# Four edits to a hybrid decoder block on one core: where NSA's masks are added, the layout of compression's tokens, the first transfers, and mLSTM's values

## The chip, the cores and the metric

The kernel runs on one core of a Trainium2 chip. The engines are PE (TensorE, matmuls), ACT (ScalarE), DVE (VectorE), POOL (GpSimd) and SP (SyncE, which here only issues transfers). The metric is the time of one execution in device microseconds; the time given is the median of three runs.

## The reference

One layer of a decoder block in fp32: 256 tokens of width 1024, 256 memory tokens. Three mixers run on the normalised input, their outputs are gated, summed and projected, and a SwiGLU channel mixer follows.

```
z = rmsnorm(x) @ w_in                      # q, 6 x kv, gates, mLSTM's q k v, merge gates
# NSA: 16 heads of 64 in 4 groups; three softmaxes for each head and token
kc, vc = compress(k0), compress(v0)        # 15 overlapping blocks of 32 tokens: silu(blocks @ w1 + pe) @ w2
o_cmp = softmax(q kc^T masked: block's end <= token) vc
o_slc = softmax(q k1^T masked: causal) v1  # 4 selection blocks, top 16: all of them
o_win = softmax(q k2^T masked: causal) v2  # the window of 512 covers all 256 tokens
y_nsa = g0 o_cmp + g1 o_slc + g2 o_win
# mLSTM, 4 heads of 128: a gated linear attention, num / max(|den|, exp(-m)), rms-normed per head
# memory cross-attention: 4 heads of 128 over rmsnorm(mem) @ w_mem_kv
y = sum_b sigmoid(merge_b) * (y_b @ w_proj_b);  x = x + rmsnorm(y @ w_out)
x = x + rmsnorm((silu(h @ w_gate) * (h @ w_up)) @ w_down),  h = rmsnorm(x)
```

## The kernel before, in words

fp32 products are made of three matmuls in fp32r: each operand is split into a high part (`whi`, `hh`, written by ACT) and the rest (`wlo`, `hl`, by DVE), and hi x hi, hi x lo and lo x hi are added in PSUM. The weights come in 162 units of 512 KB (`raw`, four buffers), each split once (`split`), so ACT and DVE each have a pass of 1024 columns for every unit.

All instructions are first recorded by `Plan` and then put in order by its own list scheduler, one fixed order for each engine. `Plan.cost` gives each instruction a duration in ns; a DVE pass costs 71 + 1.04 ns a column, whatever its operation. Priorities, `FIRST`, and a search over small shifts set the order; all profile lines therefore carry the line of `issue` (L597), and rows are told apart by tile names.

The start: SP issues the gain and first chunk of the memory (`m0`, 264 columns), the first weight unit, further chunks (`memt`) and units. Ten fp32 matmuls on ones (`warm_up`) run meanwhile, two records each. Then eight chunks of 128 channels of the memory's keys (`mem_k`) are multiplied, each with four matmuls for each of the three products (`kps`, shown as `pd<-mh,whi` and so on). `HEAD` says in how many pieces a unit's split is made.

Compression (`ph`): for keys and values (j = 0, 1) the tile `st` holds the 4 groups' tokens one after the other on 64 partitions and the same shifted by one token on the other 64. For each of 16 pairs of positions one plain fp32 matmul loads 80 columns of it at a step of 16 tokens and moves 128 columns of `w1`; the result lies token-major, is copied by ACT (`hs`), transposed by PE (`pht`), and goes on to the silu.

NSA's softmax (`nsa_half(g, tb)`, 4 groups and two halves of 128 tokens): for each of 4 heads PE makes the scores `sc` of the three branches, 272 columns for the first half, 272 and 256 in two banks for the second (16 compressed, then selected and window keys), each from two matmuls. The masks are added on PE, as matmuls of the bf16 identity (`identb`) with the bf16 mask: one of 272 columns for a head's first half, three (128, 16 and 128) for its second. DVE then takes three maxima for each head (`mx`), ACT the three exponentials with their sums, DVE scales them, PE transposes (`ptn`), ACT and DVE split (`pTh`, `pTl`), and PE multiplies by the values (`pvn`). Two heads share one scaling. Between the halves other tasks are recorded as filling: mLSTM's projections, its heads and the merge gates.

mLSTM's heads (`ml_head`): the weights `sh`, `sl` (hi and lo) of two token blocks times the values; `vml` holds values hi and values lo in separate planes, each of 128 columns and two of ones (which give the denominator). The second token block has two source blocks, so a head takes 3 x 3 matmuls of 130 columns into `pn`.

Of the kernel before, what the change touches and what calls it, by code (L numbers as in the profile page):

```python
# [12 lines left out]
F32 = mybir.dt.float32  # L13
# [14 lines left out]
N_UNITS = 162  # L28
HEAD = (2, 2, 1, 1)
# [9 lines left out]
K_ID, K_TRI, K_RV, K_BM, K_M0, K_C1, K_MT, K_END = 0, 128, 256, 257, 261, 533, 549, 677  # L39
# [5 lines left out]
class View:  # L45
# [21 lines left out]
    def rearrange(self, pattern, **sizes):  # L67
# [12 lines left out]
        assert [n for g in sides[0] for n in g] == [n for g in sides[1] for n in g]  # L80
# [6 lines left out]
        ix = self.ix.reshape([math.prod(sizes[w] for w in g) for g in sides[1]])  # L87
# [80 lines left out]
class Plan:  # L168
# [68 lines left out]
    def cost(op):  # L237
# [40 lines left out]
    FIRST, DRAIN, PLACE = 5000.0, 4000.0, 200.0  # L278
# [322 lines left out]
def block_kernel(ctx, tc, order, xN, xT, memN, memT, cst, vec, row, wg, w1, w2, W, out):  # L601
# [151 lines left out]
    memt = bigt("G", 3, [P, KD, S], F32, "memt")  # L753
# [11 lines left out]
    m0 = work.tile([P, KD + S], F32, tag="sq", bufs=3, name="m0")  # L765

    def mem_in(k):
        gain = m0[:, k:k + 1]
        src = memt[:, k, :] if k else m0[:, KD:]
        ACT.activation(mh[:, k, :], src, AF.Copy, scale=gain)  # L770
# [3 lines left out]
    def keep_k(i, ps):  # L774
# [7 lines left out]

    fetch(("mem_k", 0))
    dma(out=m0, in_=memT[:, 0:KD + S])
    mem_dma = lambda a, b: dma(out=memt[:, a:b, :], in_=memT[:, KD + a * S:KD + b * S].rearrange(
        "p (k s) -> p k s", k=b - a))
    mem_dma(1, 4)
    fetch(("mem_k", 1))
    mem_dma(4, 8)
    warm_up(10)  # L790
# [3 lines left out]
    for u in range(4):  # L794
        if ("mem_k", u) not in ready:
            fetch(("mem_k", u))
        raw = ready.pop(("mem_k", u))
# [54 lines left out]
    mraw = work.tile([P, K_END - K_M0], F32, tag="sq", bufs=3, name="mraw")  # L852
# [7 lines left out]
    dma(out=mraw, in_=cst[:, K_M0:])  # L860
# [5 lines left out]
    msk = one.tile([P, 416], BF16, name="msk")  # L866
    DVE.tensor_copy(msk, mraw)
    M0, MC1, MT, MD = msk[:, 0:272], msk[:, 272:288], msk[:, 288:416], msk[:, 0:P]
# [4 lines left out]
    for j in range(2):  # L873

        sf = bigt("E", 2, [P, 5 * S + 32], F32, f"st{j}")
        st = sf[:, 0:5 * S].rearrange("p (g t) -> p g t", g=5)
        POOL.memset(sf[:, 4 * S:], 0.0)
        POOL.memset(st[64:128, 0:4, S - 1:S], 0.0)
        POOL.tensor_copy(sf[:, 4 * S:4 * S + 32:2], vc[:, V_PEK + 16 * j:V_PEK + 16 * j + 16])
# [5 lines left out]
        ph = ps_v([80, P], "ph")  # L885
        for l in range(16):
            PE.matmul(ph, sf[:, 2 * l:2 * l + 16 * 79 + 1:16], w1t[j][:, l, :], start=(l == 0), stop=(l == 15))
        hs = work.tile([80, P], F32, tag="junk", bufs=2, name="hs")
        ACT.activation(hs, ph, AF.Copy)
        pht = ps_t([P, 80], "pht")  # L890
        PE.transpose(pht, hs, cs[0:80, K_ID:K_ID + 80])
        bias = work.tile([P, 1], F32, tag="b1", bufs=2, name="cbias")
        DVE.tensor_copy(bias, pht[:, 64:65])
        ACT.activation(hid[:, j, :, 0:NCMP], pht[:, 0:64].rearrange("p (g n) -> p g n", g=NG)[:, :, 0:NCMP], AF.Silu,
# [189 lines left out]
    vml = bigt("G", 3, [P, 2, 2, 4, P + 2], F32R, "vml")  # L1084
# [439 lines left out]
```

## Time and profile before

| | |
|---|---|
| runs | 549.79, 551.13, 549.82 us; median 549.82 |
| profiled execution | 550.37 us, its span from first to last instruction 548.6 us |
| granted clock of TensorE | 0.998 over the span |
| busy: PE, DVE, ACT, POOL | 539.8, 411.6, 343.0, 26.5 us |
| transfers | 97.8 MB, 178 GB/s on the mean |

Rows of the profile have start and duration in us, engine, line, operation, output<-inputs, shapes and count. A matmul's duration reaches from its start until its last result, and the next one starts long before that. PEld is PE's loading of weights. Waits are named by the engine that released them.

### The profile page before, as it was taken

Reading aid. Unit: us, or ns where it says so; the run is one execution under the profiler, and the core shown is the slowest. Engines: PE = TensorE matmul, PEld = TensorE weight load, DVE = VectorE, ACT = ScalarE, POOL = GpSimd, SP = SyncE. Lnnn points to the kernel's source line nnn. Section 1 sums busy time; section 2 is a strip of 40 time slices with the busy share of each in tenths; the row PEclk is TensorE's granted clock in tenths of the full one; section 3 lists DMA queues with packets and bytes.
Section 4 is the critical chain, followed back from the end, with each engine's and each line's share of the span. In section 5 each row is a group of like instructions: output and inputs, shape, how many; then the busy total and the mean of one; then the engine's idle time right before and its main releaser. Section 6 shows DMA issues by size and latency. Waiting matters only on the chain.

```text
span 548.6 us, 8855 instructions
## 1 busy us (share of the span) xinstructions
PE 539.8 (98%) x3194; PEld 474.8 (87%) x3194; DVE 411.6 (75%) x799; ACT 343.0 (63%) x676; POOL 26.5 (5%) x43
## 2 busy tenths in 40 slices
PE   9999999999999999999999999999999999999995
PEld 8899998998989889889888888788888888888884
DVE  5795696699989898987878697975777777754543
ACT  7684696576699775965896444754555555553431
POOL 0000000010020111102110000000000000000000
PEclk9999999999999999999999999999999999999999
DMA  8995326526323445345345565654455555555512
GB/s 312 416 396 198 114 107 202 194 79 229 116 79 116 147 176 178 115 154 193 112 157 177 206 217 191 226 173 148 159 192 193 191 189 184 192 185 182 189 70 76
DMA packets 28699, 97.80 MB, mean 178 GB/s; under 512 B 3312, under 2 KB 5488, under 8 KB 28400
## 3 DMA queue, kind: packets, MB, share of 16 engines
q1 hardware_dynamic: 28656, 97.24, 49.7%
q8 instruction: 25, 0.41, 0.3%
q14 instruction: 18, 0.15, 0.1%
HBM read 95.13 MB, written 1.05 MB: 175 GB/s over the span
## 4 chain that ended last, share of the span: by engine, by line
PE 91%; ACT 3%; DMA 2%; DVE 1%; issue 1%; POOL 1%; DVEq 0%; SPq 0%; ACTq 0%
PE pd L597 48%; PE pss L597 30%; PE sc L597 3%; PE pvn L597 2%; DMA raw<-in_W 2%; PE ph L597 2%; PE ptn L597 2%; ACT whi L597 1%; PE pn L597 1%; PE psm L597 1%; PE pgf L597 1%; PE pvm L597 1%; POOL ce L597 1%; PE ptx L597 0%; ACT L597 0%
## 5 line engine op out<-in xcount | busy, mean ns | idle before, releaser
L597 DVE TENSOR_TENSOR wlo<-raw,whi 128x1024 fp32r<-128x1024 f32 (+1 forms) x160 | 194.6, 1222 | 85.7 <-ACT whi L597 84.0
L597 ACT ACTIVATE whi<-raw 128x1024 fp32r<-128x1024 f32 (+1 forms) x160 | 167.3, 1049 | 131.8 <-PE pd L597 65.7
L597 PE MATMUL pd<-hh,wlo 128*128 128x256 f32 x208 | 59.6, 286 | 0.0
L597 PE MATMUL pd<-hl,whi 128*128 128x256 f32 x208 | 59.5, 286 | 0.0
L597 PE MATMUL pd<-hh,whi 128*128 128x256 f32 x208 | 59.3, 285 | 0.0
L597 PE MATMUL pd<-wlo,hh 128*128 128x512 f32 x144 | 58.4, 406 | 0.0
L597 PE MATMUL pd<-whi,hh 128*128 128x512 f32 x144 | 58.2, 404 | 0.0
L597 PE MATMUL pd<-whi,hl 128*128 128x512 f32 x144 | 57.0, 401 | 0.0
L597 PE MATMUL pss<-xc,whi 128*128 128x512 f32 x168 | 43.2, 392 | 0.0
L597 PE MATMUL pss<-whi,u 128*128 128x512 f32 x132 | 42.4, 392 | 0.0
L597 PEld LDWEIGHTS pd<-hh,whi 128*128 128x128 f32 x208 | 39.7, 191 | 0.4 <-DVE on L597 0.2
L597 PEld LDWEIGHTS pd<-hl,whi 128*128 128x128 f32 x208 | 39.8, 191 | 0.1
L597 PEld LDWEIGHTS pd<-hh,wlo 128*128 128x128 f32 x208 | 39.7, 191 | 0.1
L597 PEld LDWEIGHTS pss<-xc,whi 128*128 128x128 f32 x168 | 30.7, 189 | 5.4
L597 PE MATMUL pd<-xc,whi 128*128 128x512 f32 x120 | 31.9, 394 | 0.0
L597 PEld LDWEIGHTS pd<-wlo,hh 128*128 128x128 f32 x144 | 27.2, 189 | 4.4
L597 PEld LDWEIGHTS pd<-whi,hl 128*128 128x128 f32 x144 | 27.2, 189 | 4.3
L597 PEld LDWEIGHTS pd<-whi,hh 128*128 128x128 f32 x144 | 27.2, 189 | 4.2
L597 PEld LDWEIGHTS pss<-whi,u 128*128 128x128 f32 x132 | 24.8, 188 | 5.5
L597 ACT ACTIVATE pp<-sc,mx 128x128 f32<-128x128 f32 (+1 forms) x64 | 26.8, 431 | 1.0 <-DVE mx L597 0.8
L597 DVE TENSOR_REDUCE mx<-sc 128x1 f32<-128x16 f32 (+2 forms) x96 | 22.8, 288 | 6.1 <-PE sc L597 5.9
L597 PE MATMUL pss<-wlo,u 128*128 128x512 f32 x66 | 25.9, 392 | 0.0
(334 smaller groups left out, 1129.9 us busy)
## 6 DMA issues: line engine op xcount, KB each, us to landing
raw<-in_W SPq DMA_DIRECT2D x162, 512.0 KB, 3.2
w<-in_w SPq DMA_DIRECT2D x2, 1024.0 KB, 7.6
xn<-in_xN SPq DMA_DIRECT2D x2, 512.0 KB, 7.3
xt<-in_xT SPq DMA_DIRECT2D x2, 512.0 KB, 8.7
mn<-in_memN SPq DMA_DIRECT2D x2, 512.0 KB, 8.2
kk<-kk SPq DMA_DIRECT2D x8, 128.0 KB, 3.3
x<-in_xN SPq DMA_DIRECT2D x2, 512.0 KB, 3.7
memt<-in_memT SPq DMA_DIRECT2D x1, 512.0 KB, 7.6
```

The source lines that it names most:

```text
L597: op.ins_ = getattr(op.real, op.method)(*map(arg, op.a), **{k: arg(x) for k, x in op.kw.items()})
```

## The change

Four edits, and two planner constants (`FIRST`, the cost of an fp32 matmul).

- NSA's masks: the mask matmuls go. The masks stay in fp32 in SBUF (`msk`), and each of the three reductions of a head becomes one `tensor_tensor_reduce` on DVE, which writes -(score + mask) over the score in PSUM and the minimum of it to `mx`; the exponential uses scale -1.
- Compression: `st` is laid out with the position within a block outermost, so that 80 tokens stand at step 1. `w1` is loaded, the tokens move, the result has the hidden width on the partitions, and the copy `hs` and the transpose `pht` go. ACT's copies into `st` become four of 256 columns for each of keys and values, and DVE's shifted copies two (960 and 63 columns).
- First transfers: gain, first memory chunk and first weight unit are joined with the rest of the memory in one array (`head`), fetched in four pieces; the first has 776 columns. Two warm-ups fewer, the first chunk's hi part on DVE, the order of the three products changed.
- mLSTM: values hi, ones, values lo stand side by side (258 columns), so that `sh` meets all of them in one matmul; the lo part is added by DVE after a copy by ACT.

```diff
-K_ID, K_TRI, K_RV, K_BM, K_M0, K_C1, K_MT, K_END = 0, 128, 256, 257, 261, 533, 549, 677
+K_ID, K_TRI, K_RV, K_BM, K_M0, K_MC, K_MT, K_END = 0, 128, 256, 257, 261, 645, 677, 805
-HEAD = (2, 2, 1, 1)
+HEAD = (2, 2, 2, 1)
...
-                return max(2.05 * op.a[1].n, n / 0.6 + 10)
+                return max(1.72 * op.a[1].n, n / 0.6 + 10)
-    FIRST, DRAIN, PLACE = 5000.0, 4000.0, 200.0
+    FIRST, DRAIN, PLACE = 4300.0, 4000.0, 200.0
...
+    mt = bigt("KK", 1, [P, 3080], F32, "memt")
+    part = lambda a, b: dma(out=mt[:, a:b], in_=head[:, a:b])
...
-        ACT.activation(mh[:, k, :], src, AF.Copy, scale=gain)
+        if k == 0:
+            DVE.tensor_scalar(mh[:, k, :], src, gain, None, op0=ALU.mult)
+        else:
+            ACT.activation(mh[:, k, :], src, AF.Copy, scale=gain)
...
-    fetch(("mem_k", 0))
-    dma(out=m0, in_=memT[:, 0:KD + S])
-    mem_dma(1, 4)
+    part(0, 776)
+    part(776, 1544)
     fetch(("mem_k", 1))
-    mem_dma(4, 8)
-    warm_up(10)
+    part(1544, 2056)
+    fetch(("mem_k", 2))
+    part(2056, 3080)
+    warm_up(8)
...
-            for i, (x, y) in enumerate(((w[0], mh), (w[1], mh), (w[0], ml))):
+            for i, (x, y) in enumerate(((w[0], mh), (w[0], ml), (w[1], mh))):
...
+        st = bigt("E", 2, [P, 16, 96], F32, f"st{j}")
...
         for e in range(2):
-            ACT.activation(st[0:64, e:4:2, 0:S], ps[64 * e:64 * e + 64], AF.Copy)
-            DVE.tensor_copy(st[64:128, e:4:2, 0:S - 1], st[0:64, e:4:2, 1:S])
+            for i in range(2):
+                g = 2 * i + e
+                ACT.activation(st[0:64, :, 16 * g:16 * g + 16],
+                               ps[64 * e:64 * e + 64, i].rearrange("p (n l) -> p l n", n=16), AF.Copy)
+        DVE.tensor_copy(st[64:128, 0:15, 0:64], st[0:64, 1:16, 0:64])
+        DVE.tensor_copy(st[64:128, 15, 0:63], st[0:64, 0, 1:64])
-            PE.matmul(ph, sf[:, 2 * l:2 * l + 16 * 79 + 1:16], w1t[j][:, l, :], start=(l == 0), stop=(l == 15))
-        ACT.activation(hs, ph, AF.Copy)
-        PE.transpose(pht, hs, cs[0:80, K_ID:K_ID + 80])
+            n = l // 8
+            PE.matmul(ph, w1t[j][:, l, :], st[:, 2 * l % 16, n:n + 80], start=(l == 0), stop=(l == 15))
...
-            for i, (sb, c0) in enumerate(pieces):
-                mm3(pn[:, tb, :], sh[:, c0:c0 + P], sl[:, c0:c0 + P], vml[:, 0, sb, h, :], vml[:, 1, sb, h, :],
-                    i == 0, i == len(pieces) - 1)
-        DVE.tensor_copy(num[:, :, h, :], pn[:, :, 0:P])
+        PE.matmul(pn[:, 0:130], sh[:, 0:P], vml[:, 0, h, 0:130], start=True, stop=False, skip_group_check=True)
+        PE.matmul(pn[:, 0:P], sh[:, 0:P], vml[:, 0, h, 130:], start=False, stop=False, skip_group_check=True)
+        PE.matmul(pn[:, 0:130], sl[:, 0:P], vml[:, 0, h, 0:130], start=False, stop=False, skip_group_check=True)
+        for sb, c0 in ((0, P), (1, S)):
+            PE.matmul(pn[:, 130:388], sh[:, c0:c0 + P], vml[:, sb, h, :], start=False, stop=False,
+                      skip_group_check=True)
+            PE.matmul(pn[:, 130:260], sl[:, c0:c0 + P], vml[:, sb, h, 0:130], start=False, stop=sb == 1,
+                      skip_group_check=True)
+        DVE.tensor_copy(num[:, 0, h, :], pn[:, 0:P])
+        ACT.activation(num[:, 1, h, :], pn[:, 260:388], AF.Copy)
+        DVE.tensor_add(num[:, 1, h, :], pn[:, 130:258], num[:, 1, h, :])
...
-                    PE.matmul(s[:, 0:272], identb, M0, start=False, stop=True)
-                    PE.matmul(s[:, 0:P], identb, MD, start=False, stop=False, skip_group_check=True)
-                    PE.matmul(s[:, 256:272], identb, MC1, start=False, stop=True, skip_group_check=True)
-                    PE.matmul(s2[:, P:256], identb, MD, start=False, stop=True, skip_group_check=True)
-                for b in range(3):
-                    DVE.tensor_reduce(mx[:, j, b:b + 1], sc[b], axis=AX.X, op=ALU.max, negate=True)
+                for b, (x, y) in enumerate(sc):
+                    DVE.tensor_tensor_reduce(out=x, in0=x, in1=y, scale=-1.0, scalar=3.0e38, op0=ALU.add, op1=ALU.min,
+                                             accum_out=mx[:, j, b:b + 1])
-                    exps.append(ACT.activation(out, sc[b], AF.Exp, bias=mx[:, j, b:b + 1],
+                    exps.append(ACT.activation(out, sc[b][0], AF.Exp, scale=-1.0, bias=mx[:, j, b:b + 1],
```

## Rows read from the trace of the kernel before

**Rows 1.** The page's busy times (engine, us, share of the span, count) and the chain of work that ended last, by engine.

```profile
PE 539.8 (98%) x3194; PEld 474.8 (87%) x3194; DVE 411.6 (75%) x799; ACT 343.0 (63%) x676; POOL 26.5 (5%) x43
...
PE 91%; ACT 3%; DMA 2%; DVE 1%; issue 1%; POOL 1%; DVEq 0%; SPq 0%; ACTq 0%
```

**Rows 2.** Busy time by stretch. Columns: stretch, its length, busy us (count) of PE, PEld, DVE, ACT, POOL, then granted clock, share of the DMA engines, GB/s.

```profile
16.00:40.00 24.00, 24.00 (x157) 21.88 (x156) 19.54 (x37) 17.71 (x30) 2.59 (x8) 1.00 1.03 408
40.00:56.00 16.00, 16.00 (x125) 15.81 (x124) 8.65 (x16) 8.17 (x14) 0.39 (x2) 1.00 0.55 195
107.00:183.00 76.00, 75.23 (x519) 68.38 (x519) 69.51 (x166) 57.41 (x143) 5.45 (x7) 1.00 0.37 132
183.00:280.00 97.00, 97.00 (x602) 84.42 (x601) 82.57 (x233) 71.01 (x196) 13.23 (x11) 1.00 0.44 154
```

**Rows 3.** PE in order of time, around the masks of a first half (107 us) and of a second half (145 us). Columns: start, duration from the first start to the last end, operation, count.

```profile
107.29 0.41 PE L597 MATMUL sc<-kk,qs 128*128 128x272 f32 x2
107.55 0.29 PE L597 MATMUL sc<-msk,identb 128*128 128x272 bf16 x1
107.58 0.37 PE L597 MATMUL pd<-hl,whi 128*128 128x256 f32 x1
107.79 0.28 PE L597 MATMUL pd<-hh,wlo 128*128 128x256 f32 x1
...
145.01 0.41 PE L597 MATMUL sc<-kk,qs 128*128 128x272 f32 x2
145.26 0.24 PE L597 MATMUL sc<-msk,identb 128*128 128x128 bf16 x2
145.36 0.47 PE L597 MATMUL pd<-whi,hh 128*128 128x512 f32 x1
145.67 0.39 PE L597 MATMUL sc<-kk,qs 128*128 128x256 f32 x2
145.90 0.23 PE L597 MATMUL sc<-msk,identb 128*128 128x128 bf16 x1
145.94 0.47 PE L597 MATMUL pd<-wlo,hh 128*128 128x512 f32 x1
146.25 0.39 PE L597 MATMUL pd<-whi,hl 128*128 128x512 f32 x1
```

**Rows 4.** The reductions as one group of the page (busy us, mean ns, idle time before); the one DVE pass with an input of 128 columns from PSUM and one from SBUF (min/median/max ns); and in order of time an exponential's accumulator on ACT and two operations on DVE.

```profile
L597 DVE TENSOR_REDUCE mx<-sc 128x1 f32<-128x16 f32 (+2 forms) x96 | 22.8, 288 | 6.1 <-PE sc L597 5.9
...
L597 DVE TENSOR_TENSOR cl<-ptc,ch x8: 279/283/292, 117.8 to 285.0; 128x128 f32<-128x128 f32 x8
...
109.72 0.19 ACT L597 ACTIVATION_READ_ACCUMULATOR pc<-sc,mx 128x1 f32 x1
109.81 0.36 ACT L597 ACTIVATE pp<-sc,mx 128x128 f32<-128x128 f32 x1
...
111.80 0.15 DVE L597 TENSOR_TENSOR sm<-sm,og 128x6 f32<-128x6 f32 x1
111.87 0.28 DVE L597 TENSOR_REDUCE mx<-sc 128x1 f32<-128x128 f32 x1
```

**Rows 5.** Compression in order of time: its 32 records for the keys and what follows them; a transpose and what follows it; ACT's and DVE's copies for the values, and the values' records; and, later, plain fp32 records with 128 columns loaded and 64 moving.

```profile
39.29 4.64 PE L597 MATMUL ph<-w,st 128*80 128x128 f32 x32
43.68 0.36 PE L597 MATMUL pd<-hl,whi 128*128 128x256 f32 x1
...
45.67 0.23 PE L597 MATMUL pht<-cs,hs 80*128 80x80 f32 x1
...
45.90 0.28 PE L597 MATMUL pgf<-hh,gw 128*128 128x256 f32 x1
...
46.10 1.21 ACT L597 ACTIVATE st<-pd 64x512 f32<-64x512 f32 x2 [0.92 <-PE pd L597]
...
47.27 0.75 DVE L597 COPY st<-st 64x510 f32<-64x510 f32 x2
...
49.37 4.59 PE L597 MATMUL ph<-w,st 128*80 128x128 f32 x32
...
72.96 1.00 PE L597 MATMUL pvc<-w2t,hrep 128*128 128x64 f32 x8
73.80 0.39 PE L597 MATMUL ptx<-cs,pp 128*128 128x128 f32 x2
```

**Rows 6.** PE in order of time: the first of one mLSTM head's nine value matmuls, and what follows the last.

```profile
179.62 0.33 PE L597 MATMUL pn<-vml,sh 128*128 128x130 f32 x2
...
180.57 0.44 PE L597 MATMUL pd<-whi,hl 128*128 128x512 f32 x1
```

**Rows 7.** The start in order of time, with the idle time before and what ended it.

```profile
3.95 0.51 ACT L597 ACTIVATE mh<-m 128x256 fp32r<-128x256 f32 x1 [1.31 <-DMA m<-in_memT]
4.50 0.48 DVE L597 SCALAR_TENSOR_TENSOR ml<-m,mh 128x256 fp32r<-128x256 f32 x1 [4.50 <-ACT mh L597]
5.15 1.15 ACT L597 ACTIVATE whi<-raw 128x512 fp32r<-128x512 f32 x2 [0.69 <-DMA raw<-in_W]
5.83 1.17 PE L597 MATMUL pd<-mh,whi 128*128 128x256 f32 x4 [0.21 <-ACT whi L597]
6.84 0.63 PE L597 MATMUL pd<-mh,wlo 128*128 128x256 f32 x4
7.30 0.64 PE L597 MATMUL pd<-ml,whi 128*128 128x256 f32 x4
```

More of the change, by code (lines that the diff above doesn't have):

```diff
@@ L27 @@
 KF = FF // P
-N_UNITS = 162
-HEAD = (2, 2, 1, 1)
+N_UNITS = 161
+HEAD = (2, 2, 2, 1)
 FILL = (5, 7, 1, 1, 1, 1, 1, 1)
@@ L79, in rearrange @@
             sides.append(groups)
-        assert [n for g in sides[0] for n in g] == [n for g in sides[1] for n in g]
+        names, to = ([n for g in side for n in g] for side in sides)
         sizes = dict(sizes)
@@ L600, in block_kernel @@
 @with_exitstack
-def block_kernel(ctx, tc, order, xN, xT, memN, memT, cst, vec, row, wg, w1, w2, W, out):
+def block_kernel(ctx, tc, order, xN, xT, memN, head, cst, vec, row, wg, w1, w2, W, out):
     plan = Plan(tc)
@@ L763, in block_kernel @@
     rmb = one.tile([P, S], F32, tag="bcs", name="rmb")
-    m0 = work.tile([P, KD + S], F32, tag="sq", bufs=3, name="m0")
     def mem_in(k):
-        gain = m0[:, k:k + 1]
-        src = memt[:, k, :] if k else m0[:, KD:]
-        ACT.activation(mh[:, k, :], src, AF.Copy, scale=gain)
+        gain = mt[:, k:k + 1]
+        src = mt[:, 8:264] if k == 0 else mt[:, 1032 + k * S:1288 + k * S]
+        if k == 0:
+            DVE.tensor_scalar(mh[:, k, :], src, gain, None, op0=ALU.mult)
+        else:
+            ACT.activation(mh[:, k, :], src, AF.Copy, scale=gain)
         DVE.scalar_tensor_tensor(ml[:, k, :], src, gain, mh[:, k, :].bitcast(F32),
@@ L794, in block_kernel @@
     for u in range(4):
-        if ("mem_k", u) not in ready:
+        if u and ("mem_k", u) not in ready:
             fetch(("mem_k", u))
-        raw = ready.pop(("mem_k", u))
+        raw = ready.pop(("mem_k", u)) if u else mt[:, 264:1288]
         w = [wpool.tile([P, 1024], F32R, tag=t, bufs=4, name=t) for t in ("whi", "wlo")]
@@ L851, in block_kernel @@
     dma(out=wgt, in_=wg)
-    mraw = work.tile([P, K_END - K_M0], F32, tag="sq", bufs=3, name="mraw")
+    msk = one.tile([P, K_END - K_M0], F32, name="msk")
     w1t = [bigt("G", 3, [P, 16, P], F32, f"w1_{j}") for j in range(2)]
@@ L859, in block_kernel @@
     dma(out=cs[:, P:], in_=cst[:, P:K_M0])
-    dma(out=mraw, in_=cst[:, K_M0:])
+    dma(out=msk, in_=cst[:, K_M0:])
     dma(out=rw, in_=bass.AP(tensor=row.tensor, offset=row.offset, ap=[[0, P], [1, 520]]))
@@ L865, in block_kernel @@
     DVE.tensor_copy(identb, ident)
-    msk = one.tile([P, 416], BF16, name="msk")
-    DVE.tensor_copy(msk, mraw)
-    M0, MC1, MT, MD = msk[:, 0:272], msk[:, 272:288], msk[:, 288:416], msk[:, 0:P]
+    mtb = one.tile([P, P], BF16, name="mtb")
+    DVE.tensor_copy(mtb, msk[:, K_MT - K_M0:])
+    MC, MT = [msk[:, 384 + 16 * i:400 + 16 * i] for i in range(2)], mtb
     hid = one.tile([P, 2, NG, 32], F32, name="hid")
@@ L1187, in nsa_half @@
                     PE.matmul(s[:, 0:272], q, kh[:, g, P:400], start=True, stop=False)
-                    PE.matmul(s[:, 0:272], q, kl[:, g, P:400], start=False, stop=False)
-                    PE.matmul(s[:, 0:272], identb, M0, start=False, stop=True)
-                    sc = (s[:, P:144], s[:, 0:P], s[:, 144:272])
+                    PE.matmul(s[:, 0:272], q, kl[:, g, P:400], start=False, stop=True)
+                    sc = ((s[:, P:144], MC[0]), (s[:, 0:P], msk[:, P:256]), (s[:, 144:272], msk[:, P:256]))
                 else:
@@ L1490, in _layout @@
     cst[:, K_BM:K_BM + 4] = (i[:, None] // 32) == np.arange(4)[None, :]
-    arrs = {"xN": a["x"][0], "xT": xT, "memN": a["mem"][0], "memT": memT, "cst": cst, "vec": vec, "row": row, "wg": wg, "w1": w1, "w2": w2}
+    memT = ft(a["mem"][0].T).reshape(P, KD * S)
+    head = np.concatenate([a["g_mem"][0].reshape(KD, P).T, memT[:, 0:S], units["mem_k", 0], memT[:, S:]], axis=1)
+    arrs = {"xN": a["x"][0], "xT": xT, "memN": a["mem"][0], "head": head, "cst": cst, "vec": vec, "row": row, "wg": wg, "w1": w1, "w2": w2}
     return {k: np.ascontiguousarray(v) for k, v in arrs.items()}, units
```

50 lines of the change are left out of this document (21 added, 29 removed).

## The prediction

> **What bounds the kernel now.** I read the busy times first: PE is busy 98% of the span, every other engine 75% or less [rows 1]. A busy share alone proves little, because matmul ends are modelled, so I read the chain of waits next: 91% of it is PE's own work [rows 1]. Then the windows. From 16 to 280 us PE has no idle time in the stretches shown, except 0.8 us between 107 and 183 [rows 2]. The reader is to see that PE is the queue everything else is hidden behind, and that a matmul taken out of it shortens the kernel by its own slot, unless another engine then falls behind. The candidate is DVE: 69.5 of 76 us from 107 to 183 and 82.6 of 97 from 183 to 280 [rows 2]. That is where NSA's softmax runs.
>
> A matmul's slot is not its duration in the rows (some 0.28 us for 256 columns): matmuls overlap, and the slot is the distance between starts. All sums on PE below use distances between starts.
>
> **Masks (PE loses 64 matmuls).** In the first half of a group, two score matmuls, one mask of 272 columns and one projection matmul take 107.29 to 107.79, 0.50 us; the next projection matmul follows at its usual 0.12 [rows 3]. Two score matmuls are 0.13 each (107.29 to 107.55) and the projection 0.12, so the mask costs 0.12 to 0.13. Its own start-to-start is only 0.03 us (107.55 to 107.58); the rest shows as a late start of the matmul behind it. For the second half, 145.01 to 145.67 holds two score matmuls, two masks and a projection of 512 columns: 0.66 less 0.25 less 0.23 leaves 0.18. 145.67 to 146.25 has one mask: 0.58 less 0.24 less 0.23 leaves 0.11 [rows 3]. So a head's first half costs 0.125 and its second 0.29; 16 of each are 16 x 0.415 = 6.6 us. Where three masks stand in a row they share one switch, and where a mask stands alone it costs a little more than here, so the bounds are 6.0 and 7.3. I take 6.8.
>
> **The same masks on DVE.** 96 reductions become 96 passes with two inputs, an output and an accumulated minimum. No row of before has such a pass. For the stream itself the nearest rows agree that a second input is free: two inputs of 128 columns from PSUM and SBUF take 283 ns, and the 96 reductions, of 16, 128 and 256 columns in equal numbers, 133 on the mean, take 288 ns on the mean [rows 4]. What the accumulator costs I take from ACT, whose accumulating passes are followed by an instruction of their own: 109.72 to 109.81, 0.09 us each [rows 4]. DVE's smallest operation lets the next one start 0.07 us later (111.80 to 111.87) [rows 4]. I take 0.08 x 96 = 7.7 us of extra DVE time. The lower bound is 0 (the minimum written with the pass); the upper one a whole further pass of the same length, 22.8 us for the 96 [rows 4].
>
> Does it fit? From 107 to 280 DVE is busy 152.1 of 173 us [rows 2]. PE's stretch becomes 173 - 6.8 - 0.7 (mLSTM, below) = 165.5. DVE would be at 152.1 + 7.7 + 0.3 = 160.1 of it. On average it still fits, by 5 us; at the upper bound it does not (175.2). It will not be free either. The planner prices the new pass as it priced the reduction, so it places PE's transposes behind a pair of heads as if the six passes took their old time. They come 6 x 0.08 = 0.5 us late, and what waits is first ACT's exponentials, then the scaling on DVE, then the transposes on PE, whose order is fixed, with all projections behind them. There are 16 pairs. If each showed in full it would be 7.7 us; if all were absorbed by slack, nothing. I take 0.1 us for each, 1.6 us, nearer the low end, because PE hardly waits for DVE now although DVE is as busy as 91% from 107 to 183 [rows 2]. The passes also write PSUM where the reductions only read; a wait between two passes on one bank would lie in the same bounds.
>
> **Compression (32 matmuls turned round, two transposes gone).** In plain fp32 each matmul is two records. For the keys 32 records run from 39.29 to 43.68, 4.39 us, 0.137 each [rows 5]. The weights loaded there are 80 columns at a step of 16 elements. After the change the weights are 128 plain columns and 80 columns move. The nearest row is the second projection of the compressed values, fp32, 128 plain columns loaded, 64 moving: 8 records in 72.96 to 73.80, 0.105 each [rows 5]. So 64 x (0.138 - 0.108) = 1.9 us; bounds 1.0 (0.122 each) and 2.2. The transposes: 45.67 to 45.90 is one of them and a 256-column matmul of 0.12, so 0.11 each, 0.2 us for two.
>
> ACT's copies into the staging tile become eight of 256 instead of four of 512, reading PSUM at a step of 16. From 40 to 56 us ACT is busy 8.2 and DVE 8.7 of 16 us [rows 2], and the gate projection, 24 matmuls from 45.90 on, lies between the values' copy (ACT 46.10) and their matmuls at 49.37 [rows 5]. I cost it at nothing; that cover is gone once the chain grows by over 1.3 us (DVE's copies end at 48.02, the matmuls start at 49.37 [rows 5]). [...]
>
> **mLSTM (9 matmuls of a head become 7).** One head's nine run from 179.62 to 180.57, 0.95 us, 0.106 each [rows 6]. Five stay at that, and the two of 258 columns should cost what 256 do, 0.12 [rows 3]: 0.53 + 0.24 = 0.77. That is 0.18 x 4 = 0.7 us, bounds 0.4 and 0.9. DVE's copy of 256 becomes a copy and an addition of 128 each, about 0.07 more a head, and ACT gains one copy; 0.3 us of DVE in all, counted above.
>
> **First transfers.** Now PE starts on data at 5.83: the 132 KB of the first chunk are seen at 3.95, the first 512 KB unit at 5.15 (512 KB in 1.20 us), and the first half of its split takes until 5.83 [rows 7]. The new first transfer holds 776 columns, 388 KB: 3.95 + 256/512 x 1.20 = 4.55, and first matmul at 5.23, 0.6 earlier. But the first four matmuls take 1.01 us (5.83 to 6.84) and the next four 0.46 [rows 7], the first at half the speed. If PE's speed rises at the same moment after, the 0.6 us are filled at half rate and worth 0.3. I take 0.3. Bounds: 0.6 at the top; at the bottom -0.5, if with two fewer warm-up matmuls the rise comes 1 us later. Behind it DMA is full until 40 us [rows 2] and carries the same bytes, so a gain larger than this would be taken back there. The first chunk's hi part moves from ACT to DVE, which is idle until 4.50 [rows 7]; the second product of each chunk now needs its lo part, which DVE makes before the weights' lo half: both at nothing, as four matmuls at half speed lie between. The wider mask constants (65 KB more) and their smaller cast lie behind projections.
>
> **The sum.** 6.8 + 1.9 + 0.2 + 0.7 + 0.3 - 1.6 = 8.3 us. The profiled execution took 550.4; that gives 542.1. The median of the runs lies 0.55 below it, so I forecast 541.5.
>
> **The rivals.**
> - *DVE becomes the bound in NSA.* At 0.15 us a pass (the full duration of a small DVE operation [rows 4], or a shorter read with a wait between passes on one bank) the extra is 14.4 us and DVE would be busy 166.8 of 165.5. PE then waits 1 us for the mean and, as each of 16 pairs comes 0.9 us late and now nothing makes it up, an estimated third of 14.4 for the bursts: 9.9 - 6 = 4 gained, 546. For it: DVE is the fullest engine there. Against: the planner can move projections. Chance 0.17.
> - *The step-16 reads stall compression.* If ACT's copies take four times their time, the values' 1.2 us become 4.8, the 1.3 us of cover is passed by 2.3, and the keys' likewise by some 1 us: 544.5 to 545. Chance 0.08.
> - *The masks on DVE cost more than PE saves: slower.* It needs PE to wait over 9.9 us, so DVE above 165.5 + 9.9 = 175.4 us for the stretch, 23 more than now: 0.24 us or more a pass, a second full-length stream over the scores. At 0.3 us the extra is 28.8 us and the time 549.8 + 15.7 - 9.9 = 555.6. Nothing in the rows shows DVE at two cycles a column. Chance 0.04.
> - *No net change*: the same mechanism between 0.21 and 0.24 a pass. Chance 0.04.
>
> **The numbers.** My forecast has the remaining chance, 0.67, with its own range 539 to 543.5: with no lateness at all and the upper bounds of the other terms it would be 549.8 - 11.2 = 538.6; with twice the lateness and the middle of the other terms 543.1. To leave out no more than 2 in 10 the range must reach into the first two rivals: 538.9 to 545.6. Two runs of before agree within 0.03 us and the third is 0.25% off, so under 0.3% (1.6 us) counts as no change. Faster 0.92, same 0.04, slower 0.04.
>
> **What would show it.** Right: no mask records in the scores; score matmuls followed by projections at 0.13 and 0.23; the compression's records at 0.105 to 0.11; PE busy some 9 us less, and no PE wait for DVE longer than 0.5 us. The passes on DVE at 0.08, 0.20 and 0.33 between starts, plus one short read each. Wrong: DVE above 95% from 107 to 270 and PE idle behind the transposes; the first data matmul at 5.8 as before or the slow matmuls lasting beyond 7 us; ACT's copies at 0.5 us or more.

## The result and the profile after

The changed kernel takes 542.44 us (median of four runs, 542.07 to 543.06) against 550.42 for the kernel before on the same chip: a ratio of 0.9855, 95% interval 0.9839 to 0.9871, so 8.0 us faster. The prediction was 541.5 with a range of 538.9 to 545.6. The profiled execution took 542.5, its span is 540.7 (548.6 before).

Three lines of the page, which answer to [rows 1] and to the group of reductions in [rows 4] (busy us, share and count by engine; the chain by engine; the passes that add the mask, busy us and mean ns, idle time before):

```profile
PE 530.9 (98%) x3116; PEld 464.9 (86%) x3116; DVE 414.2 (77%) x900; ACT 340.8 (63%) x682; POOL 30.2 (6%) x43
...
PE 79%; DVE 9%; ACT 5%; DMA 4%; issue 2%; POOL 1%; SPq 0%; DVEq 0%; ACTq 0%
...
L598 DVE CUSTOM_DVE_ANT_0 sc<-sc,msk 128x16 f32<-128x16 f32 (+2 forms) x96 | 27.2, 316 | 4.2 <-PE sc L598 3.4
```

PE has 78 records less and 8.9 us less busy time; it is still 98% busy, but its share of the chain falls from 91% to 79%, and DVE's rises from 1% to 9%. The same stretches as in [rows 2], with the same columns:

```profile
16.00:40.00 24.00, 23.84 (x154) 21.37 (x153) 20.05 (x36) 17.89 (x33) 4.78 (x10) 1.00 1.03 415
40.00:56.00 16.00, 16.00 (x138) 15.85 (x138) 8.21 (x15) 10.29 (x16) 0.12 (x1) 1.00 0.51 182
107.00:183.00 76.00, 75.11 (x492) 67.07 (x491) 71.45 (x219) 58.18 (x153) 6.03 (x8) 1.00 0.38 131
183.00:280.00 97.00, 97.00 (x586) 84.76 (x585) 85.92 (x283) 74.23 (x197) 15.28 (x13) 1.00 0.45 159
```

DVE has more work in both NSA stretches, yet PE waits there hardly more than before. PE's waits from 20 us on, first before the change and then after it (what waited and for whom, us in total, times, longest):

```profile
PE ptc L597 <- DVE pTl L597: 0.4, 1, 0.4
PE pvn L597 <- POOL ce L597: 0.4, 1, 0.4
PE pss L597 <- ACT xc L597: 0.2, 1, 0.2
```

```profile
PE pd L598 <- DVE on L598: 0.9, 1, 0.9
PE pss L598 <- ACT xc L598: 0.5, 1, 0.5
PE ptx L598 <- DVE xg L598: 0.3, 1, 0.3
PE pvn L598 <- POOL ce L598: 0.3, 1, 0.3
PE rbc L598 <- POOL rm L598: 0.2, 1, 0.2
```

What the passes look like on DVE (start, duration, operation):

```profile
106.67 0.18 DVE L598 CUSTOM_DVE_ANT_0 sc<-sc,msk 128x16 f32<-128x16 f32 x1
106.76 0.14 DVE L598 DVE_READ_ACCUMULATOR2_ANT mx<- 128x1 f32 x1
106.76 0.33 DVE L598 CUSTOM_DVE_ANT_0 sc<-sc,msk 128x128 f32<-128x128 f32 x1
107.01 0.14 DVE L598 DVE_READ_ACCUMULATOR2_ANT mx<- 128x1 f32 x1
107.01 0.34 DVE L598 CUSTOM_DVE_ANT_0 sc<-sc,msk 128x128 f32<-128x128 f32 x1
...
107.75 0.23 DVE L598 CUSTOM_DVE_ANT_0 sc<-sc,msk 128x16 f32<-128x16 f32 x1
107.85 0.19 DVE L598 DVE_READ_ACCUMULATOR2_ANT mx<- 128x1 f32 x1
108.07 0.30 DVE L598 CUSTOM_DVE_ANT_0 sc<-sc,msk 128x128 f32<-128x128 f32 x1
108.29 0.14 DVE L598 DVE_READ_ACCUMULATOR2_ANT mx<- 128x1 f32 x1
108.46 0.30 DVE L598 CUSTOM_DVE_ANT_0 sc<-sc,msk 128x128 f32<-128x128 f32 x1
108.68 0.14 DVE L598 DVE_READ_ACCUMULATOR2_ANT mx<- 128x1 f32 x1
```

Two things are to be seen. The read of the accumulator is there, but a pass that does not wait starts at the same moment as the read: its slot is then nothing. And a pass that follows one on the same bank waits: after 16 columns 0.32 or 0.28 instead of 0.09 (107.75 to 108.07), after 128 columns 0.39 instead of 0.22 (108.07 to 108.46). It waits for that read: it starts 0.03 us after the read has ended (107.85 and 0.19 make 108.04, then 108.07), and the trace's record of such a pass names DVE's own semaphore (45 of the 96 passes do; with the output in SBUF, below, one). So the wait comes from an order that the program asks for between two passes on one PSUM tile; whether the chip needs it was not tested. Nineteen passes wait so, some 0.18 us each, 3.4 us in all. The planner puts another bank's pass between them where it can, and then they stand 0.25 apart (106.76 to 107.01). Over all 96, the median distance from a pass to the read behind it is 94, 217 and 350 ns for 16, 128 and 256 columns; from a reduction to the next operation it was 84, 198 and 332 before.

PE where two score matmuls stand alone, where its longest wait for DVE between 105 and 268 us lies, and at the start (answers to [rows 3] and [rows 7]):

```profile
4.61 1.22 PE L598 MATMUL pd<-mh,whi 128*128 128x256 f32 x4
5.63 1.05 PE L598 MATMUL pd<-ml,whi 128*128 128x256 f32 x4
6.48 0.74 PE L598 MATMUL pd<-mh,wlo 128*128 128x256 f32 x4
7.06 0.63 PE L598 MATMUL pd<-mh,whi 128*128 128x256 f32 x4
...
104.98 0.42 PE L598 MATMUL sc<-kk,qs 128*128 128x272 f32 x2
105.23 0.28 PE L598 MATMUL pd<-hh,whi 128*128 128x256 f32 x1
105.35 0.28 PE L598 MATMUL pd<-hl,whi 128*128 128x256 f32 x1
...
158.84 0.39 PE L598 MATMUL pd<-hh,whi 128*128 128x256 f32 x1 [0.88 <-DVE on L598]
```

Two scores and a projection take 0.37 us (104.98 to 105.35) where before they took 0.50 with the mask between them [rows 3]. Compression's 32 records for the keys run from 39.24 to 42.81, 0.112 each (0.137 in [rows 5]).

### The profile page after: what moved, and what is told of

It is laid out like the page before. It is cut to its first block, busy times and chain, and to the rows that moved or that the text cites. A ratio compares the mean times of both kernels' runs of the same rounds, so it can differ in the third digit from the quotient of the medians.

```text
span 540.7 us, 8802 instructions
## 1 busy us (share of the span) xinstructions
PE 530.9 (98%) x3116; PEld 464.9 (86%) x3116; DVE 414.2 (77%) x900; ACT 340.8 (63%) x682; POOL 30.2 (6%) x43
## 4 chain that ended last, share of the span: by engine, by line
PE 79%; DVE 9%; ACT 5%; DMA 4%; issue 2%; POOL 1%; SPq 0%; DVEq 0%; ACTq 0%
PE pd L598 41%; PE pss L598 27%; DMA raw<-in_W 4%; DVE wlo L598 2%; PE pvn L598 2%; PE sc L598 2%; ACT whi L598 1%; PE ptn L598 1%; PE ph L598 1%; DVE cy L598 1%; ACT L598 1%; DVE sc L598 1%; DVE xt L598 1%; PE psm L598 1%; PE pgf L598 1%
## 5 line engine op out<-in xcount | busy, mean ns | idle before, releaser
L598 DVE TENSOR_TENSOR wlo<-raw,whi 128x1024 fp32r<-128x1024 f32 (+1 forms) x159 | 191.7, 1210 | 83.8 <-ACT whi L598 82.4
L598 DVE CUSTOM_DVE_ANT_0 sc<-sc,msk 128x16 f32<-128x16 f32 (+2 forms) x96 | 27.2, 316 | 4.2 <-PE sc L598 3.4
```

What stands on the lines that cost most here:

```text
L598: op.ins_ = getattr(op.real, op.method)(*map(arg, op.a), **{k: arg(x) for k, x in op.kw.items()})
```

## The experiments

Ratios are to the kernel before, run beside each. The changed kernel itself was measured three times in effect: 0.9855, and 0.9851 and 0.9842 in two variants below that leave its work as it is; 0.985 is taken as its ratio, and a ratio's third decimal is 0.55 us. Each experiment is an edit of the changed kernel.

**Each edit taken back.** The first three diffs show the core.

```
-                    PE.matmul(s[:, 0:272], q, kl[:, g, P:400], start=False, stop=True)
+                    PE.matmul(s[:, 0:272], q, kl[:, g, P:400], start=False, stop=False)
+                    PE.matmul(s[:, 0:272], identb, M0, start=False, stop=True)
...
-                    DVE.tensor_tensor_reduce(out=x, in0=x, in1=y, scale=-1.0, scalar=3.0e38, op0=ALU.add, op1=ALU.min,
-                                             accum_out=mx[:, j, b:b + 1])
+                    DVE.tensor_reduce(mx[:, j, b:b + 1], sc[b], axis=AX.X, op=ALU.max, negate=True)
```

> The changed kernel with NSA's masks back on PE (64 mask matmuls, 96 plain reductions), the three other edits kept. Theory (the masks are worth what their slots on PE were, less PE's new waits for DVE): the changed kernel took 542.4; scores and masks together have 3.4 us more slots and the projections behind them 1.9 us, less 0.8 to 1.2 us of waits that the changed kernel has on PE: 546.5 to 547, PE's waits over 150 ns near 2.6 us as in the kernel before instead of 3.9. The prediction's own terms, 6.8 - 1.6, give 547.6. Rival (the pass on DVE gives most of it back, DVE is the bound): 544 to 545.

Measured: 545.71, ratio 0.9910 (0.9897 to 0.9924), 3.3 us above the changed kernel (2.6 to 4.1 by the interval). The prediction's net of 5.2 is too large, my theory's 4.1 to 4.6 at the edge, the rival's 1.6 to 2.6 too small. On PE, I added up every run of score matmuls, from its first start to the start of the second matmul behind it, less what the planner takes for each matmul (columns / 2.4 + 13 ns; for 256 columns 0.12 us, as from 105.23 to 105.35 above): 6.7 us before, 6.6 here, 1.0 in the changed kernel. So 5.6 to 5.7 us really left PE, and some 2 of them did not reach the end. PE's waits over 150 ns (starts that come later than that price allows by more than 150 ns) are 3.7 us here and 3.9 in the changed kernel, not the 2.6 that I expected: this order has waits of its own.

```
-            PE.matmul(ph, w1t[j][:, l, :], st[:, 2 * l % 16, n:n + 80], start=(l == 0), stop=(l == 15))
+            PE.matmul(ph, sf[:, 2 * l:2 * l + 16 * 79 + 1:16], w1t[j][:, l, :], start=(l == 0), stop=(l == 15))
```

> The changed kernel with compression as before (tokens loaded at a step of 16, result transposed), the rest kept. Theory: 64 records at 0.137 instead of 0.112 between starts and two transposes more, 1.7 + 0.2 = 1.9 us: 544.3. Rival (the chain around compression has slack elsewhere, or the weights arriving until 40 us set the pace, so that the gain comes back as a wait): 542.4 to 543, with PE's records as slow as before and a wait of over 0.5 us gone elsewhere between 16 and 80.

Measured: 544.68, ratio 0.9893 (0.9878 to 0.9909), 2.4 us above. The records take 8.94 us from start to start here and 7.19 in the changed kernel. The theory's 1.9 lies within the interval; the rival's half microsecond does not.

```
-            PE.matmul(pn[:, 130:388], sh[:, c0:c0 + P], vml[:, sb, h, :], start=False, stop=False,
-                      skip_group_check=True)
...
+                mm3(pn[:, tb, :], sh[:, c0:c0 + P], sl[:, c0:c0 + P], vml[:, 0, sb, h, :], vml[:, 1, sb, h, :],
+                    i == 0, i == len(pieces) - 1)
```

> The changed kernel with mLSTM's values in two planes as before (nine matmuls a head), the rest kept. Theory: 0.77 us more slots on PE: 543.2. Rival (the copy by ACT and the addition by DVE that the edit adds in a stretch where DVE is over 0.9 full cost as much as PE gains): 542.4 or below.

Measured: 546.61, ratio 0.9919 (0.9906 to 0.9931), 3.8 us above: neither theory nor rival. The matmuls `pn` take 3.76 us of slots here and 3.08 in the changed kernel, as expected, but PE's waits over 150 ns are 5.8 us instead of 3.9, in other places. The planner had made a wholly different order of this kernel. The two order experiments below follow from it.

```
-    part(0, 776)
-    part(776, 1544)
+    fetch(("mem_k", 0))
+    dma(out=m0, in_=memT[:, 0:KD + S])
...
-    warm_up(8)
+    warm_up(10)
```

> The changed kernel with the first transfers as before (132 KB, then the first unit; ten warm-ups, hi x hi, lo, planner's FIRST of 5000), the rest kept. Theory from the trace of the changed kernel (first data matmul 4.61 instead of 5.83, full speed from 6.7 in both, so six more slow matmuls done by then, 6 x 0.12, plus part of a wait): 0.9 us: 543.3. The prediction's term: 0.3 us, 542.7. Rival (the transfers are full until 40 us and carry the same bytes, so the head start is waited away there): 542.4, with a wait of PE between 16 and 40 us in the changed kernel (0.44 us at 31.3) that is gone here.

Measured: 544.01, ratio 0.9876 (0.9862 to 0.9889), 1.4 us above. The theory's 0.9 lies within the interval (0.7 to 2.1), the prediction's 0.3 below it; the planner's `FIRST` was taken back too, and with it the order. The traces tell more than the times here (the start, below).

**What an order is worth.**

```
-    MATMUL, SLACK, PASSES, ROUNDS = (10.0, 13.3), (60.0, 130.0), 3, 40
+    MATMUL, SLACK, PASSES, ROUNDS = (10.0, 13.3), (130.0,), 3, 40
```

> The changed kernel, nothing left out or added, put in another order by the planner (its trials confined to a slack of 130 ns). It prices the luck of an order. Theory (the result without mLSTM's edit, 3.5 us slower instead of 0.8, is mostly another order's waits): 543 to 546, with the same slots of PE's kinds of matmul and other waits. Rival (orders hardly matter, the parts' prices are the edits' own): 542.4 within 0.5.

> The changed kernel with mLSTM's values in two planes as before, in another order (planner's trials confined to a matmul overhead of 10 ns). Theory (the edit is worth its 0.77 us of slots, the rest of the 3.5 us seen without it was the order's waits): below 546, down to 543.2, with at least 1 us less of PE's waits than in the first order (5.8 us over 150 ns). Rival (the edit itself is worth 3 us or more, as its nine matmuls meet something that the slots don't show): 546 to 547 again.

Measured: the changed kernel in the other order 542.30, ratio 0.9851 (0.9829 to 0.9873), no different, as the rival said; without mLSTM's edit in another order 544.00, ratio 0.9886 (0.9858 to 0.9915), 2.0 us above the changed kernel where the first order gave 3.8, with PE's waits over 150 ns down from 5.8 to 3.5 us. So one to two microseconds can be the order alone, and what an edit is worth can't be read from one pair of kernels more closely than that. mLSTM's edit is worth 0.7 in slots; the times allow that (the last interval reaches down to 0.4 above) and don't show it. Taken back one at a time, the four edits cost 3.3, 2.4, 2.0 to 3.8 and 1.4 us, 9 to 11 together, more than the 8.0 that they gain together: the times of single edits do not add up.

**Is DVE the bound?**

```
-                    DVE.tensor_tensor_reduce(out=x, in0=x, in1=y, scale=-1.0, scalar=3.0e38, op0=ALU.add, op1=ALU.min,
-                                             accum_out=mx[:, j, b:b + 1])
+                    DVE.tensor_add(x, x, y)
+                    DVE.tensor_reduce(mx[:, j, b:b + 1], x, axis=AX.X, op=ALU.max, negate=True)
```

> The changed kernel with each of its 96 passes as two instructions on DVE: an addition of the mask over the score in PSUM, then the reduction as before the change (the planner prices both). Theory by the prediction's rule (DVE at 152.1 + 23 + 0.3 us of a stretch of 165.5, PE waits for the excess and for a third of the bursts, 9.9 + 7.7, less the 6.8 + 0.7 that PE gains there and 3.1 elsewhere... the rule's own result is 549 to 550): DVE over 95% from 107 to 270 and PE waiting there 8 us or more. Rival (DVE has more slack than its busy share says, since the short waits between two passes on one bank, 0.17 us each, are already paid and the planner moves projections into the gaps): 544 to 546, PE's waits over 150 ns at most 5 us.

Measured: 543.16, ratio 0.9867 (0.9845 to 0.9888), 0.9 us above the changed kernel. The two groups of this kernel's page, and its busy times by stretch (columns as in [rows 2]):

```profile
L598 DVE TENSOR_TENSOR sc<-sc,msk 128x16 f32<-128x16 f32 (+2 forms) x96 | 26.1, 295 | 1.1 <-PE sc L598 0.7
...
L598 DVE TENSOR_REDUCE mx<-sc 128x1 f32<-128x16 f32 (+2 forms) x96 | 25.7, 286 | 0.2
```

```profile
107.00:183.00 76.00, 74.76 (x492) 67.36 (x491) 73.53 (x192) 56.87 (x134) 6.33 (x7) 1.00 0.39 130
183.00:270.00 87.00, 86.81 (x521) 75.76 (x521) 85.11 (x279) 65.97 (x194) 13.37 (x11) 1.00 0.43 148
```

A whole second pass for each of the 96, 19.6 us by the medians of their distances (83, 199 and 332 ns, 32 of each), costs 0.9 us (-0.3 to 2.1 by the interval); the time lies under the rival's bracket too. DVE's busy time on the page is 428.1 us against 414.2 in the changed kernel and 411.6 before, so 13.9 and 16.5 more; it is 97 and 98% busy there and PE still 98 and nearly 100%. PE's waits over 150 ns are 2.9 us from 107 to 270, not the 8 of the theory, and 5.6 in all, a little over the rival's 5. The theory by the prediction's rule (549 or more) falls, and with it the rival that DVE becomes the bound. Not all of the room was there before: the scores, whose first and last start this line gives,

```profile
L598 PE MATMUL sc<-kk,qs x96: 276/287/393, 106.1 to 273.6; 128*128 128x272 f32 x64, 128*128 128x256 f32 x32
```

take 167.5 us here and 162.7 in the changed kernel, and the work of PE behind them is 5.2 us shorter. The planner moved projections in among NSA's softmax (18 more matmuls of 512 columns between the first and the last score, three fewer of 256), so PE stayed full while DVE took longer. It did know the price here; the prediction's lateness was for passes whose price it does not know.

**The step in PSUM.**

```
-                ACT.activation(st[0:64, :, 16 * g:16 * g + 16],
-                               ps[64 * e:64 * e + 64, i].rearrange("p (n l) -> p l n", n=16), AF.Copy)
+                ACT.activation(st[0:64, :, 16 * g:16 * g + 16].rearrange("p l n -> p n l"),
+                               ps[64 * e:64 * e + 64, i].rearrange("p (n l) -> p n l", n=16), AF.Copy)
```

> The changed kernel, its order the same instruction by instruction, with the step of 16 in ACT's eight copies into the staging tile moved from the read of PSUM to the write in SBUF (step 96 there). Theory (a read of PSUM at a step costs ACT nothing that counts): the eight copies take 0.37 us as before, 0.28 between starts, the time is the changed kernel's, 542.1 to 542.6. Rival (the step costs ACT time, hidden so far): copies shorter by 0.05 us or more. Since nothing else differs, this run is also the changed kernel measured once more beside the next two.

Measured: 541.99, ratio 0.9842 (0.9829 to 0.9856). ACT's copies into `st`, min/median/max ns, first in the changed kernel, then here:

```profile
L598 ACT ACTIVATE st<-pss x4: 368/373/383, 35.4 to 36.3; 64x256 f32<-64x256 f32 x4
```

```profile
L598 ACT ACTIVATE st<-pss x4: 651/670/709, 35.4 to 37.0; 64x256 f32<-64x256 f32 x4
```

Reading PSUM at a step of 16 costs nothing that counts, as the theory said: a copy of 256 plain columns from PSUM takes 363 ns in the changed kernel,

```profile
L598 ACT ACTIVATE join<-pss 128x256 f32<-128x256 f32 x21 | 7.6, 363 | 1.2 <-PE pss L598 1.2
```

the mean of that group. But the edit was not the same work without the step, as I had meant it: writing SBUF at a step of 96 costs 0.3 us for 256 columns. The time doesn't move, so compression has room for 8 x 0.3 us of ACT too.

**Where the pass writes.** If the waits between passes on one bank cost something, the output may go elsewhere: into the SBUF tile in which the exponentials will stand (`o`).

```
-                    DVE.tensor_tensor_reduce(out=x, in0=x, in1=y, scale=-1.0, scalar=3.0e38, op0=ALU.add, op1=ALU.min,
+                    o = pc[:, 2 * pr + j, 0:16] if b == 0 else pv4[:, j, b - 1]
+                    DVE.tensor_tensor_reduce(out=o, in0=x, in1=y, scale=-1.0, scalar=3.0e38, op0=ALU.add, op1=ALU.min,
...
-                    exps.append(ACT.activation(out, sc[b][0], AF.Exp, scale=-1.0, bias=mx[:, j, b:b + 1],
+                    exps.append(ACT.activation(out, out, AF.Exp, scale=-1.0, bias=mx[:, j, b:b + 1],
```

> The changed kernel with the pass writing its output into the SBUF tile in which the exponentials will stand, instead of over the score in PSUM (ACT then reads and writes that tile in place). Theory: in the changed kernel a pass on the bank that the pass before it wrote starts 0.39 us after it instead of 0.22, and this is what makes PE's waits for DVE longer (3.9 us over 150 ns in all, 2.6 before); with the output elsewhere the wait is gone, the banks come free earlier, and the time is 541 to 541.8. Rival (those waits are filled by DVE's other work or are needed for the accumulator anyway; PE's waits come from the order): 542.4 within 0.6, passes on one bank still 0.39 apart.

Measured: 539.68, ratio 0.9801 (0.9780 to 0.9823): 2.7 us under the changed kernel, 1.3 below the theory's bracket, and the fastest kernel of this study. Its passes on DVE:

```profile
106.62 0.17 DVE L598 CUSTOM_DVE_ANT_0 pc<-sc,msk 128x16 f32<-128x16 f32 x1
106.72 0.08 DVE L598 DVE_READ_ACCUMULATOR2_ANT mx<- 128x1 f32 x1
106.72 0.29 DVE L598 CUSTOM_DVE_ANT_0 pp<-sc,msk 128x128 f32<-128x128 f32 x1
106.93 0.08 DVE L598 DVE_READ_ACCUMULATOR2_ANT mx<- 128x1 f32 x1
106.93 0.29 DVE L598 CUSTOM_DVE_ANT_0 pp<-sc,msk 128x128 f32<-128x128 f32 x1
```

Passes on one bank follow at 0.10 and 0.21, and of the 96 only one still names DVE's semaphore. But its order is another one, so two more kernels were run: the same in another order, and one in which only two of a head's three passes write to SBUF, so that its first bank is held as before.

```
-                for b, (x, y) in enumerate(sc):
+                for b, (x, y) in ((1, sc[1]), (2, sc[2]), (0, sc[0])):
+                    o = pv4[:, j, b - 1] if b else x
```

> The kernel whose passes write to SBUF (539.7, 2.4 us under the changed kernel), in another order (planner's trials confined to a matmul overhead of 13.3 ns). Theory (the gain comes from where the pass writes): 539 to 541, at least 1 us under the changed kernel. Rival (the gain was a lucky order): 541.5 or more.

> As the kernel whose passes write to SBUF, but the pass of 16 compressed columns comes third and still writes over its scores in PSUM, so that a head's first bank is held until ACT's exponential, as in the changed kernel, while two passes on one bank no longer wait for each other (one wait in the second half's banks at most). Theory A (the wait between passes on one bank is what cost): 539.5 to 540.5. Theory B (the earlier release of the score banks is what helps): 541.5 to 542.5, with PE's waits near the changed kernel's. Both in part: between.

Measured: the other order 542.04, ratio 0.9840 (0.9825 to 0.9855), which by its expectation speaks for the rival, a lucky order; two of three passes 540.35, ratio 0.9814 (0.9801 to 0.9828), which would be theory A, though with some waits between passes left (0.33 us between starts after four passes of 128 columns, 0.46 after four of 256). Times in different orders could not settle it. The last kernel keeps the order: the output of a pass (`first`) is moved to SBUF (`out`) after the order is made, where the earlier users of that place (`old`) come before the pass:

```
+        for first, exp, out in self.pairs:
...
+            if all(at[op] < at[first] for op in old):
+                first.kw["out"] = out
+                first.tiles.append(out.tile)
+                exp.a = (out, out, *exp.a[2:])
```

> The changed kernel in its own order, instruction for instruction; 72 of its 96 passes write into the SBUF tile of the exponentials, the other 24 (those whose SBUF tile is not free so early in this order) over the score in PSUM as in the changed kernel. It separates the place of the output from the order, which the kernels with SBUF passes so far (539.7, 540.35, 542.0 in three orders, against 542.0 to 542.4 in three runs with PSUM passes) did not. Theory (the place itself shortens the time, by ending waits between passes on one bank and freeing banks earlier): 540.3 to 541.2. Rival (the place alone does nothing in a fixed order; what the faster kernels gained is an order that uses it, or luck): 541.7 to 542.5, the wait of PE at 157.8 (1.15 us, for DVE's copy behind the passes) still there.

Measured: 540.79, ratio 0.9819 (0.9796 to 0.9843), inside the theory's bracket, with an interval that just misses 0.985 and overlaps the contiguous read's, so the time alone does not decide. The trace is sharper. The score matmuls' first and last start, in the changed kernel, in the kernel with the contiguous read (same order, same passes), and in this one:

```profile
L598 PE MATMUL sc<-kk,qs x96: 274/287/396, 105.0 to 267.7; 128*128 128x272 f32 x64, 128*128 128x256 f32 x32
```

```profile
L598 PE MATMUL sc<-kk,qs x96: 274/287/398, 105.1 to 267.9; 128*128 128x272 f32 x64, 128*128 128x256 f32 x32
```

```profile
L610 PE MATMUL sc<-kk,qs x96: 276/288/375, 104.9 to 266.5; 128*128 128x272 f32 x64, 128*128 128x256 f32 x32
```

162.7 and 162.8 us against 161.6. All 3116 PE records can be set side by side, as the order is one: against the changed kernel the contiguous read is later by 0.07 to 0.16 us all the way from 105 to 268 us, while this kernel goes from 0.03 to 1.21 us earlier, in seven steps of 0.1 to 0.3. So the place alone is worth 1.2 us there in a fixed order. Not all of it lasts: at the last matmul the lead is 1.0 us over the changed kernel's profile and 0.4 over the contiguous read's.

Five of the seven steps stand at score matmuls. One of them, on ACT and PE in the changed kernel, then on PE here:

```profile
108.60 0.21 ACT L598 ACTIVATION_READ_ACCUMULATOR pp<-sc,mx 128x1 f32 x1
...
108.86 0.52 PE L598 MATMUL sc<-kk,qs 128*128 128x272 f32 x2
109.22 0.28 PE L598 MATMUL pd<-hh,wlo 128*128 128x256 f32 x1
```

```profile
108.81 0.42 PE L610 MATMUL sc<-kk,qs 128*128 128x272 f32 x2
109.07 0.28 PE L610 MATMUL pd<-hh,wlo 128*128 128x256 f32 x1
```

In the changed kernel the scores start when ACT is through with an exponential of the scores that stood in the bank before (108.60 and 0.21 make 108.81, then 108.86), and two of them take 0.36 us; here, where ACT reads SBUF, 0.26. By the sum used for the masks, the late starts around scores fall from 1.0 us to 0.4. So about half of the 1.2 us is banks that come free earlier, and the rest was not taken apart. The wait at 157.8 stayed (0.8 us), which the theory had not said: the copy that PE waits for stands on DVE behind a 0.74 us pass of mLSTM's (`qkm`), which does not get shorter.

**The start, in all the traces.** The experiments gave 12 traces with the new start and two with the old. Old: first data matmul at 5.83 and 5.89, the third chunk at 9.21 and 9.08, the memory's keys done at 17.77 and 17.50. New: first matmul at 4.61 to 5.21 (5.03 on the mean), third chunk at 8.45 to 9.17 (8.82), keys done at 16.90 to 17.73 (17.32). The gain of 0.8 us at the first matmul has shrunk to 0.3 at the third chunk. In one trace with the new start, the contiguous read's (start, duration, operation, wait):

```profile
5.15 0.74 PE L598 MATMUL pd<-mh,whi 128*128 128x256 f32 x4 [0.54 <-ACT whi L598]
5.73 0.62 PE L598 MATMUL pd<-ml,whi 128*128 128x256 f32 x4
...
7.54 0.62 PE L598 MATMUL pd<-mh,wlo 128*128 128x256 f32 x4
8.45 0.73 PE L598 MATMUL pd<-mh,whi 128*128 128x256 f32 x4 [0.29 <-ACT whi L598]
```

PE is at full speed from 5.4 us on (0.45 us for four matmuls, 5.73 to 6.18), is through with two chunks at 8.0, and then waits for the second weight unit. In the changed kernel's own profile PE was slow until 6.7 (1.02 us for the first four, 4.61 to 5.63) and reached the third chunk at 8.48 all the same, with no wait. In nine of the 12 traces PE waits there for the second unit to land and be split, so in these that is what bounds the start; in the other three, all of them slow ones, PE comes just as the split ends. Why the matmuls are slow for longer in four of them stays open: the granted clock reads 1.00 in the changed kernel's slow stretch (5.40 to 6.70 us) as well as behind it.

## Why the prediction came out right

The total was right, 8.3 us forecast and 8.0 measured, with its terms off in both directions.

- **Masks off PE, 6.8.** Measured 5.7, under the lower bound of 6.0. The single readings were right (0.50 to 0.37 us in a first half), and so was their sum: the late starts around the scores come to 6.7 us before, where the prediction added up 6.6. That three masks in a row cost less than the same masks apart holds in the trace before: four masks, one alone and three in a row, take 0.32 us there (142.57 to 143.85, less six scores and a projection); one alone was read as 0.11 [rows 3], which leaves 0.21 for the three, where [rows 3] gives 0.29 apart. The step that failed is that all of it leaves with the masks. 1.0 us of late starts stays around scores without masks: scores that wait for ACT to free a bank (0.36 us for two at 108.86, where 0.25 is usual), and scores right behind a transpose (0.21 us for the first of them, at 193.75, 223.37 and 261.34, where 0.125 is usual).
- **DVE's price, 7.7, and its consequence, -1.6.** The price failed: 10 to 19 ns more a pass, 1.5 us for the 96, because the accumulator's read has no slot where the next pass does not wait for it. What was named as lying "in the same bounds", the wait between passes on one bank, is what came instead, 3.4 us in 19 passes: some 5 us in place of 7.7. The consequence came out near the estimate in size: PE's slots fell by 7.8 us in all, where masks 5.7, records 1.7, transposes 0.2, mLSTM 0.8 and the start 0.9 of this trace add to 9.3, so 1.4 us were given back, nearly all as PE's waits over 150 ns (3.9 us, 2.6 before). That it came near is luck, because the mechanism did not appear: the prediction had PE wait at the transposes behind a pair of heads (`ptn`). None of the waits listed above is at `ptn`. The longest is for a copy of mLSTM's, at 158.84, and `pss` and `ptx` wait at 349 and 347 us, some 70 us behind NSA's last transpose.
- **Does it fit on DVE?** The answer (yes) was right, the reason too narrow. The prediction held the stretch at 165.5 us; in the test with two passes DVE is busy 16.5 us more than before, 3 more than that stretch had left (165.5 - 152.1), and the time grows by 0.9. The planner fits more projections in among NSA, which the prediction names only as an argument against its first rival.
- **Compression, 1.9 + 0.2.** Measured 1.7 from start to start, 0.112 each where 0.108 was taken; ACT's copies that read PSUM at a step of 16 cost nothing, as put: 373 ns for 256 columns, against 363 for a copy without a step. A step cost time where it stood in the write of SBUF, 670 ns at a step of 96.
- **mLSTM, 0.7.** Measured 0.77 in slots (3.85 to 3.08).
- **First transfers, 0.3.** Measured 0.3 over the traces, mostly by another mechanism. The forecast had the first matmul at 5.23 (5.03 on the mean) and a loss in slow matmuls, which four of the 12 traces show; in the eight where PE is at full speed early it loses the same at the second unit instead. "A gain larger than this would be taken back there" was the step that held. The changed kernel's own profile, 0.9, is the luckiest of 12.
- **What would show it.** No mask records, score slots, and PE's busy time came as listed, compression's records at 0.112 just above; one PE wait for DVE is longer than the 0.5 us allowed (0.88 at 158.84), and it is there with the passes moved too.

The rivals: DVE as the bound, no change and slower fall with the measured price, 0.05 us a pass (5 us for the 96), and the two-pass kernel shows that 0.17 a pass (16.5 us) would not have made DVE the bound either; the stall of compression, at four times a copy's time, was my guess at a price, and ACT's 373 ns against 363 refute it.

## What to carry to other kernels

Before an engine is called the bound of a stretch, ask whether the planner can lengthen the stretch with other work of the engine that is: here DVE took 13.9 us more of short passes for 0.9 us of time. In this kernel a pass that writes over its PSUM input made the next pass on that bank wait for its accumulator's read (0.39 us from start to start for 128 columns, 0.21 with the output in SBUF), and an exponential that reads PSUM held the bank for the next scores (it ended at 108.81, they started at 108.86, and two took 0.36 us, 0.26 with the exponentials reading SBUF); if the consumer can read SBUF, write there: in a fixed order that gave 1.2 us around NSA here, 0.4 to 1.0 at the last matmul. Where a planner remakes the whole order, price an edit by slots in the trace or in a fixed order: the same work in another order moved by up to 2 us, more than most of these edits are worth.

## What the runs showed of the hardware

- A DVE pass with two inputs, an output and an accumulated minimum takes 10 to 19 ns more than the plain reduction from its start to what follows; its accumulator read is a record of its own of 143 ns (82 where the pass writes SBUF), but a next pass that does not wait starts with it.
- A pass that waits for DVE's own semaphore, here behind a pass that wrote the same PSUM bank, starts 0.03 us after that pass's accumulator read has ended: 0.39 us from start to start for 128 columns, 0.22 otherwise.
- ACT copies 256 fp32 columns from PSUM in 373 ns at a step of 16 and in 363 without one, and in 670 when it writes SBUF at a step of 96.
- At the start, matmuls ran at half their later rate (0.213 us between starts, later 0.118) until 5.1 to 5.4 us in eight of the 12 traces with the new start and until 6.7 to 7.0 in four; the changed kernel and the contiguous read, one order, are one of each. The granted clock reads 1.00 in the changed kernel's slow stretch.
